# Two edits in a two-block network kernel: recurrent heads' maxima spread by DMA, attention heads' scores in pairs

## The chip, the cores and the metric

The kernel runs on one core of a Trainium2 chip. The metric is device time of one execution in microseconds (us). A core has TensorE (PE; its weight loads are PEld), VectorE (DVE), ScalarE (ACT), GpSimd (POOL) and SyncE (SP), which here only issues transfers.

## The reference

Two blocks over 256 tokens of width 1024, fp32, depth 2 each. What matters here is the attention of the first block and the recurrent mixer of the second. The rest (projections, gated feed-forward, stick-breaking attention, and a product-key expert layer) is untouched.

```python
# first block, both layers: 16 heads of 64, 4 key heads, band of 128, a sink per head
sc = einsum('bqkgd,bskd->bkgqs', q, k) * scale        # masked to the band
m = maximum(max(sc), sink)
p = exp(sc - m);  denom = sum(p) + exp(sink - m)
o = einsum('bkgqs,bskd->bqkgd', p / denom, v)

# second block, layer 0: 8 recurrent heads (mLSTM), queries and keys of 64, values of 128
b = cumsum(log_sigmoid(f_pre))
log_d = where(causal, b[l] - b[s] + i_pre[s], -inf)
m_t = maximum(b + m_prev, max(log_d))                 # the running maximum
s_qk = einsum('bhcld,bhcsd->bhcls', q, k) * exp(log_d - m_t)
hh = (s_qk @ v + ...) / maximum(abs(den), exp(-m_t))
```

## The kernel before

The kernel is traced in the order of the Python program; a planner then orders each engine's instructions by their place in the program and by when it reckons their inputs and buffers to be ready. So on each engine a later instruction can go ahead of an earlier one that has to wait. Waits between engines are set by the planner too; two instructions that touch one PSUM bank, one writing and one reading, are kept in program order.

**Projections.** Every weight block (128x1024, 512 KB) is loaded by SP (`load`, L166, 4 buffers `raw`), split into a high part by ScalarE (L177, `whi`, 5 buffers) and a residual by VectorE (L180, `wlo`, 5 buffers), and multiplied three times (`mm3`, L185 to L187: high by high, residual by high, high by residual). `form_b` makes a 128x256 result (PSUM tile mmB, 24 matmuls of 256 columns), `form_a` two 128x512 results (mmA). There are 4 PSUM buffers for these, 2 in the pool `pt` (tag "tp") and 2 in the pool `pa` (tag "sc").

**Attention (`_first_layer`, L390 to L446).** The work is cut into eight groups a layer: two halves of the tokens by four key heads, four query heads each. `scores(t, g)` makes, head by head, three matmuls over 64 partitions (L402; an even head's operands lie in partitions 0 to 63, an odd one's in 64 to 127) and a VectorE reduction that adds the band and takes the maximum (L405, into one of 6 buffers `e`). Two consecutive heads (0 and 1, 2 and 3) share one PSUM tile sc of `pa`. `values(t, g)` takes the exponentials (L417), divides (L421), transposes (L427), splits (L429, L430) and multiplies by the values into the tile po, also of `pa`; L436 and L437 put the result into oThi and oTlo. Scores of one group are traced ahead of the values of the one before. The convolution's projections (L456 on) do not depend on the attention; the mix (L477 on) reads oThi and oTlo.

**Recurrent heads (`mlstm`, L581).** The three gate columns g3 of each head are transposed to 8 partitions, where VectorE's scans make the running maxima M (8 heads x 128 tokens, two halves, L660 to L665). Eight projections with a convolution and a SiLU make queries and keys (L674 to L684), a `form_a` the second half of the values (L698). Then `head` runs eight times: tile pe takes minus M on all 128 partitions (L705: a fp32 matmul of a one-row selector by M) plus the causal mask (L706: a bf16 identity by the mask), in the pool `pt`; three exponentials (L710) make the weights me from pe and the gates; the scores mps (L713, L714, pool `pa`) are multiplied in by VectorE (L716); the values mpo (L718 to L720, pool `pa`) are copied (L722) and squared (L724). After the heads come the output gate's projections (L744) and the output projection.

A matmul on fp32 tiles appears as two instructions, on the split tiles as one.

Of the kernel before, what the change touches and what calls it, by code (L numbers as in the profile page):

```python
# [7 lines left out]
F32 = mybir.dt.float32  # L8
BF16 = mybir.dt.bfloat16
# [3 lines left out]
AF = mybir.ActivationFunctionType  # L13
ALU = mybir.AluOpType
# [3 lines left out]
S = 256  # L18
# [15 lines left out]
NEG = -1e30  # L34


def bc(ap, shape):
    return ap.to_broadcast(shape)
# [77 lines left out]
class Net:  # L116
# [66 lines left out]
    def mm3(self, out, lhs, rhs, start, stop):  # L183
        nc = self.nc
        nc.tensor.matmul(out, lhsT=lhs[0], rhs=rhs[0], start=start, stop=False)  # L185
        nc.tensor.matmul(out, lhsT=lhs[0], rhs=rhs[1], start=False, stop=False)  # L186
        return nc.tensor.matmul(out, lhsT=lhs[1], rhs=rhs[0], start=False, stop=stop)  # L187

    def pop(self):
        self.done += 1  # L190
# [134 lines left out]
    def _first_layer(self, ctx, l, norm, nxt, setup):  # L325
        nc, tc, d = self.nc, self.tc, self.d
# [63 lines left out]
        def scores(t, g):  # L390
            mx = self.sm.tile([128, 4], F32, tag="mx", name="mx")
            nm = self.sm.tile([128, 4], F32, tag="nm", name="nm")
            sk = self.sm.tile([128, 4], F32, tag="sk", name="sk")
            dn = self.sm.tile([128, 4], F32, tag="dn", name="dn")
            scs = []
            for i in range(4):
                hh = 4 * g + i
                r0 = 64 * (hh % 2)
                if i % 2 == 0:
                    sc2 = self.pa.tile([128, 2, S], F32, tag="sc", name="sc")  # L400
                sc = sc2[:, i % 2, :]
                self.mm3(sc, [v[r0:r0 + 64, hh // 2, t * 128:(t + 1) * 128] for v in qT],  # L402
                         [v[r0:r0 + 64, g, :] for v in kT], True, True)
                e = B.tile([128, S], F32, tag="e", name="e", bufs=6)
                nc.vector.tensor_tensor_reduce(e, sc, self.band[:, t, :], 1.0, NEG, op0=ALU.add, op1=ALU.max,  # L405
                                               accum_out=mx[:, i:i + 1])
                scs.append(e)
            sv = sink[:, 4 * g:4 * g + 4]
            nc.vector.tensor_tensor(mx, mx, sv, op=ALU.max)
            nc.vector.tensor_scalar(nm, mx, -1.0, None, op0=ALU.mult)  # L410
            nc.vector.tensor_tensor(sk, sv, mx, op=ALU.subtract)
            return nm, sk, dn, scs
# [168 lines left out]
    def mlstm(self, norm, g1, nxt):  # L581
        nc, tc, d = self.nc, self.tc, self.d
        with ExitStack() as ctx:
# [11 lines left out]
            le = A.tile([128, 128], F32, name="le")  # L595
            gt = A.tile([128, 128], F32, name="gt")
            mkf = A.tile([128, 128], F32, name="mkf")
            mk = A.tile([128, 128], BF16, name="mk")
            idb = A.tile([128, 128], BF16, name="idb")
            sel = A.tile([8, 8, 128], F32, name="sel")  # L600
            nc.sync.dma_start(le, d["c_le"])
            nc.sync.dma_start(gt, d["c_gt"])
            nc.sync.dma_start(mkf, d["c_mk_gt"])
            nc.vector.tensor_copy(mk, mkf)
            nc.vector.tensor_copy(idb, self.ident)
            nc.sync.dma_start(sel, d["c_sel"])
            one = A.tile([128, 1], F32, name="one")
            nc.vector.memset(one, 1.0)

# [46 lines left out]
                nc.tensor.transpose(p3[0:8, j, :], g3[:, j, :], self.ident)  # L656
            s3 = A.tile([8, 3, 128], F32, name="s3")
            nc.vector.tensor_copy(s3, p3[0:8, 0:3, :])
            M = A.tile([8, 3, 128], F32, name="M")
            nc.vector.tensor_tensor_scan(M[:, 0, :], s3[:, 0, :], s3[:, 0, :], 0.0, op0=ALU.max, op1=ALU.max)  # L660
            in1 = A.tile([8, 1], F32, name="in1")
            nc.vector.tensor_reduce(in1, s3[:, 2, :], axis=AX.X, op=ALU.max)
            nc.vector.tensor_tensor(in1, in1, beta, op=ALU.max)
            nc.vector.tensor_tensor_scan(M[:, 1, :], s3[:, 1, :], s3[:, 1, :], in1, op0=ALU.max, op1=ALU.max)
            nc.vector.tensor_copy(M[:, 2, :], M[:, 1, :])  # L665
            em = A.tile([128, 2, 8], F32, name="em")
            p4 = self.pt.tile([128, 4, 128], F32, tag="tp", name="tp4")
            for t in range(NT):
# [32 lines left out]

            def head(hh):
                r0, c = 64 * (hh % 2), hh // 2
                pe = self.pt.tile([128, 3, 128], F32, tag="tp", name="pe")
                nc.tensor.matmul(pe, lhsT=sel[:, hh, :], rhs=M, start=True, stop=False)  # L705
                nc.tensor.matmul(pe[:, 0:3:2, :], lhsT=idb, rhs=bc(mk[:, None, :], [128, 2, 128]),  # L706
                                 start=False, stop=True)
                e = B.tile([128, 3, 128], F32, tag="me", name="me")
                for j, g in ((0, 0), (1, 2), (2, 1)):
                    nc.scalar.activation(e[:, j, :], pe[:, j, :], AF.Exp, bias=g3[:, g, hh:hh + 1])  # L710
                psx = self.pa.tile([128, 3, 128], F32, tag="sc", name="mps")
                q, k = qk[c], qk[4 + c]
                nc.tensor.matmul(psx[:, 0:2, :], lhsT=k[r0:r0 + 64, 0:128], rhs=q[r0:r0 + 64, :], start=True, stop=True)  # L713
                nc.tensor.matmul(psx[:, 2, :], lhsT=k[r0:r0 + 64, 128:256], rhs=q[r0:r0 + 64, 128:256],  # L714
                                 start=True, stop=True)
                nc.vector.scalar_tensor_tensor(e, psx, 0.125, e, op0=ALU.mult, op1=ALU.mult)  # L716
                po = self.pa.tile([128, 2, 129], F32, tag="sc", name="mpo")
                nc.tensor.matmul(po[:, 0, :], lhsT=e[:, 0, :], rhs=va[0][:, hh, :], start=True, stop=True)  # L718
                nc.tensor.matmul(po[:, 1, :], lhsT=e[:, 1, :], rhs=va[0][:, hh, :], start=True, stop=False)
                nc.tensor.matmul(po[:, 1, :], lhsT=e[:, 2, :], rhs=va[1][:, hh, :], start=False, stop=True)  # L720
                for t in range(NT):
                    nc.vector.tensor_copy(num[t][:, hh, :], po[:, t, :])  # L722
                    jk = B.tile([128, 128], F32, tag="mjk", name="mjk")
                    nc.scalar.activation(jk, po[:, t, 0:128], AF.Square, accum_out=ss[t][:, hh:hh + 1])  # L724
# [438 lines left out]
def layout(inp):  # L1163
# [54 lines left out]
    if "ma_w_in_2" in inp:  # L1218
        w = f("ma_w_in_2")
        cat["ma_w_qk"] = tile_b(w[:, :, :1024])[0]  # L1220
        cat["ma_w_vo"] = tile_a(w[:, :, 1024:3072])[0]
        wif = np.zeros((128, KD, 128), np.float32)
        wif[:, :, :16] = w[0, :, 3072:].reshape(KD, 128, 16).transpose(1, 0, 2)
        cat["ma_w_if"] = wif.reshape(128, D)
        cat["ma_conv_w"] = np.ascontiguousarray(f("ma_conv_w_2")[0].reshape(4, KD, 128).transpose(2, 1, 0).reshape(128, 4 * KD))
        cat["ma_b_if"] = f("ma_b_if_2")
        cat["ma_hnorm_g"] = f("ma_hnorm_g_2").reshape(1, D)
        cat["ma_w_out"] = tile_a(f("ma_w_out_2"))[0]
        cat["c_le"] = (p <= q).astype(np.float32)
        cat["c_gt"] = (p > q).astype(np.float32)  # L1230
        cat["c_mk_gt"] = np.where(p > q, NEG, 0.0).astype(np.float32)
        sel = np.zeros((8, 8, 128), np.float32)
        sel[np.arange(8), np.arange(8)] = -1.0
        cat["c_sel"] = sel
    if "kv_w_2" in inp:
        cat["kv_ada_w"] = np.ascontiguousarray(f("kv_ada_w_2").T.reshape(1, 16, 128, D))
        cat["kv_ada_b"] = fm(f("kv_ada_b_2")[None])
# [99 lines left out]
```

## Time and profile before

| | us |
|---|---|
| median of the timed runs (3) | 2929.24 |
| lowest, highest | 2927.11, 2933.46 |
| the profiled execution | 2919.5 |
| its span, first to last instruction | 2917.7 |

| engine | busy us | share of the span |
|---|---|---|
| TensorE matmul (PE) | 2878.2 | 99% |
| TensorE weight load (PEld) | 2589.4 | 89% |
| VectorE (DVE) | 2163.6 | 74% |
| ScalarE (ACT) | 1433.5 | 49% |
| GpSimd (POOL) | 145.3 | 5% |

Matmuls are pipelined: one appears as busy from its start to the end of its drain, and the next has started by then. So the busy share of PE only says that its queue never ran dry; what a matmul costs is the step from its start to the next one's. "PEclk" is the granted TensorE clock as a share of 2.4 GHz: 1.00 is 2.4, 0.50 is 1.2 GHz.

### The profile page before, as it was taken

Reading aid. Unit: us, or ns where it says so; the run is one execution under the profiler, and the core shown is the slowest. Engines: PE = TensorE matmul, PEld = TensorE weight load, DVE = VectorE, ACT = ScalarE, POOL = GpSimd, SP = SyncE. Lnnn points to the kernel's source line nnn. Section 1 sums busy time; section 2 is a strip of 40 time slices with the busy share of each in tenths; the row PEclk is TensorE's granted clock in tenths of the full one; section 3 lists DMA queues with packets and bytes.
Section 4 is the critical chain, followed back from the end, with each engine's and each line's share of the span. In section 5 each row is a group of like instructions: output and inputs, shape, how many; then the busy total and the mean of one; then the engine's idle time right before and its main releaser. Section 6 shows DMA issues by size and latency. Waiting matters only on the chain.

```text
span 2917.7 us, 50501 instructions
## 1 busy us (share of the span) xinstructions
PE 2878.2 (99%) x19693; PEld 2589.4 (89%) x19693; DVE 2163.6 (74%) x4179; ACT 1433.5 (49%) x2363; POOL 145.3 (5%) x54
## 2 busy tenths in 40 slices
PE   8999999999999999999999999999999999999999
PEld 7898997899897789999999887877899999988887
DVE  6886766886755576978876897686599787569865
ACT  6645445554545564453344334566544434443454
POOL 0000000000000002330000000000032200000000
PEclk9999999999999899999999999999999999999999
DMA  6385775367665345564588358753455545554564
GB/s 216 104 284 190 262 250 192 109 222 241 224 199 182 125 152 157 183 211 142 171 278 270 122 172 281 229 183 115 137 162 172 183 140 159 188 167 128 188 201 146
DMA packets 153570, 542.40 MB, mean 186 GB/s; under 512 B 20002, under 2 KB 21226, under 8 KB 153330
## 3 DMA queue, kind: packets, MB, share of 16 engines
q1 hardware_dynamic: 153330, 539.18, 57.2%
q8 instruction: 154, 2.52, 0.3%
q14 instruction: 86, 0.70, 0.1%
HBM read 538.02 MB, written 1.09 MB: 185 GB/s over the span
## 4 chain that ended last, share of the span: by engine, by line
PE 89%; DVE 8%; ACT 1%; DMA 1%; issue 1%; SPq 0%; DVEq 0%; ACTq 0%
PE acc L185 8%; PE acc L187 8%; PE acc L186 8%; PE mmB L186 7%; PE mmB L187 7%; PE mmB L185 7%; PE pA L185 6%; PE pA L186 6%; PE pA L187 6%; PE mmA L186 5%; PE mmA L187 5%; PE mmA L185 5%; PE pG L968 4%; DVE wlo L180 2%; PE sc L185 1%
## 5 line engine op out<-in xcount | busy, mean ns | idle before, releaser
L177 ACT CAST whi<-raw 128x1024 fp32r<-128x1024 f32 x893 | 936.0, 1050 | 866.9 <-PE pA L186 364.5
L180 DVE TENSOR_TENSOR wlo<-raw,whi 128x1024 fp32r<-128x1024 f32 x849 | 1048.7, 1240 | 336.5 <-ACT whi L177 332.9
L185 PE MATMUL pA<-hhi,whi 128*128 128x256 f32 x2048 | 585.6, 286 | 5.7 <-ACT act L917 4.8
L186 PE MATMUL pA<-hlo,whi 128*128 128x256 f32 x2048 | 579.2, 283 | 0.0
L187 PE MATMUL pA<-hhi,wlo 128*128 128x256 f32 x2048 | 578.9, 283 | 0.0
L186 PE MATMUL mmB<-hlo,whi 128*128 128x256 f32 x1480 | 423.2, 286 | 0.0
L187 PE MATMUL mmB<-hhi,wlo 128*128 128x256 f32 x1480 | 421.6, 285 | 0.0
L185 PE MATMUL mmB<-hhi,whi 128*128 128x256 f32 x1480 | 421.5, 285 | 0.0
L187 PE MATMUL acc<-whi,wr 128*128 128x512 f32 x1024 | 400.4, 391 | 2.6 <-DVE wr L989 2.4
L185 PEld LDWEIGHTS pA<-hhi,whi 128*128 128x128 f32 x2048 | 393.4, 192 | 9.7 <-ACT act L917 5.9
L186 PE MATMUL acc<-wlo,wr 128*128 128x512 f32 x1024 | 401.0, 392 | 0.0
L186 PEld LDWEIGHTS pA<-hlo,whi 128*128 128x128 f32 x2048 | 392.4, 192 | 2.2
L185 PE MATMUL acc<-whi,wr 128*128 128x512 f32 x1024 | 393.2, 396 | 0.0
L187 PEld LDWEIGHTS pA<-hhi,wlo 128*128 128x128 f32 x2048 | 392.2, 191 | 0.0
L186 PEld LDWEIGHTS mmB<-hlo,whi 128*128 128x128 f32 x1480 | 282.9, 191 | 4.3
L187 PEld LDWEIGHTS mmB<-hhi,wlo 128*128 128x128 f32 x1480 | 282.8, 191 | 2.3
L185 PEld LDWEIGHTS mmB<-hhi,whi 128*128 128x128 f32 x1480 | 282.9, 191 | 1.5
L988 ACT CAST wr<-act 128x256 fp32r<-128x256 f32 x256 | 103.6, 406 | 346.1 <-PE acc L186 340.9
L187 PEld LDWEIGHTS acc<-whi,wr 128*128 128x128 f32 x1024 | 192.2, 188 | 46.9 <-DVE wr L989 6.6
L186 PEld LDWEIGHTS acc<-wlo,wr 128*128 128x128 f32 x1024 | 192.6, 188 | 39.1 <-DVE wlo L180 0.6
L185 PEld LDWEIGHTS acc<-whi,wr 128*128 128x128 f32 x1024 | 193.1, 189 | 35.6 <-ACT wr L988 0.2
L537 DVE CUSTOM_DVE_ANT_0 adaw<-adaw,cb 128x1024 f32<-128x1024 f32 x112 | 136.9, 1223 | 86.4 <-DMA adaw<-in_ada_w 77.5
(357 smaller groups left out, 4063.1 us busy)
## 6 DMA issues: line engine op xcount, KB each, us to landing
raw<-in_peer_u SPq DMA_DIRECT2D x256, 512.0 KB, 3.7
raw<-in_peer_v SPq DMA_DIRECT2D x256, 512.0 KB, 4.1
adaw<-in_ada_w SPq DMA_DIRECT2D x96, 512.0 KB, 4.7
raw<-in_w_gates SPq DMA_DIRECT2D x80, 512.0 KB, 3.9
raw<-in_w_down SPq DMA_DIRECT2D x44, 512.0 KB, 3.9
raw<-in_w_gate SPq DMA_DIRECT2D x36, 512.0 KB, 4.1
raw<-in_w_up SPq DMA_DIRECT2D x36, 512.0 KB, 4.0
raw<-in_w_qkv SPq DMA_DIRECT2D x24, 512.0 KB, 4.5
```

The source lines that it names most:

```text
L177: (nc.vector.tensor_copy if FIRST_HI[i:i + 1] == "v" else nc.scalar.copy)(hi, raw)
L180: self.last_lo = lo_eng.tensor_tensor(lo, raw, hi.bitcast(F32), op=ALU.subtract)
L185: nc.tensor.matmul(out, lhsT=lhs[0], rhs=rhs[0], start=start, stop=False)
L186: nc.tensor.matmul(out, lhsT=lhs[0], rhs=rhs[1], start=False, stop=False)
L187: return nc.tensor.matmul(out, lhsT=lhs[1], rhs=rhs[0], start=False, stop=stop)
L537: nc.vector.tensor_tensor_reduce(w, w, self.csilu, 1.0, 0.0, op0=ALU.mult, op1=ALU.add, accum_out=col[:, j:j + 1])
L968: nc.tensor.matmul(pg[:, :, 4 * g + t], lhsT=e2[:, g, :, t], rhs=e1[:, j, :, t], start=(j == 0), stop=(j == 1))
L988: nc.scalar.copy(gh, row(c))
```

## The change

In the attention, a group's two score tiles are made ahead of its reductions. `mm3_pair` takes two heads at a time, one in each half of the partitions, and alternates between them; the first of each pair writes tile 0 and the second tile 1, so that a tile now holds heads 0 and 2, or 1 and 3. The four reductions follow.

In the recurrent heads, M is stored to DRAM (8 KB) and loaded back to all 128 partitions in one transfer of 1 MB (Mb); VectorE subtracts the mask once for all heads (Mm, two instructions). The exponentials read Mm and Mb in SBUF, with a scale of -1. The matmuls L705 and L706 and what fed them go: the tile sel and its load, the bf16 copies of mask and identity, the copy of M's second half. The buffers me go from 2 to 4, and mpo moves to the pool `pt`, where pe was.

```diff
+    def mm3_pair(self, outs, lhss, rhss, start, stop):
+
+        for i, (a, b) in enumerate(((0, 0), (0, 1), (1, 0))):
+            for out, lhs, rhs in zip(outs, lhss, rhss):
+                self.nc.tensor.matmul(out, lhsT=lhs[a], rhs=rhs[b], start=start and i == 0, stop=stop and i == 2)
...
             scs = []
+            sc2 = [self.pa.tile([128, 2, S], F32, tag="sc", name="sc") for j in range(2)]
+            for i in range(2):
+                rs = [slice(64 * j, 64 * j + 64) for j in range(2)]
+                self.mm3_pair([sc2[j][:, i, :] for j in range(2)],
+                              [[v[r, 2 * g + i, t * 128:(t + 1) * 128] for v in qT] for r in rs],
+                              [[v[r, g, :] for v in kT] for r in rs], True, True)
             for i in range(4):
-                hh = 4 * g + i
-                r0 = 64 * (hh % 2)
-                if i % 2 == 0:
-                    sc2 = self.pa.tile([128, 2, S], F32, tag="sc", name="sc")
-                sc = sc2[:, i % 2, :]
-                self.mm3(sc, [v[r0:r0 + 64, hh // 2, t * 128:(t + 1) * 128] for v in qT],
-                         [v[r0:r0 + 64, g, :] for v in kT], True, True)
                 e = B.tile([128, S], F32, tag="e", name="e", bufs=6)
-                nc.vector.tensor_tensor_reduce(e, sc, self.band[:, t, :], 1.0, NEG, op0=ALU.add, op1=ALU.max,
-                                               accum_out=mx[:, i:i + 1])
+                nc.vector.tensor_tensor_reduce(e, sc2[i % 2][:, i // 2, :], self.band[:, t, :], 1.0, NEG, op0=ALU.add,
+                                               op1=ALU.max, accum_out=mx[:, i:i + 1])
...
-            mk = A.tile([128, 128], BF16, name="mk")
-            idb = A.tile([128, 128], BF16, name="idb")
-            sel = A.tile([8, 8, 128], F32, name="sel")
...
-            nc.vector.tensor_copy(mk, mkf)
-            nc.vector.tensor_copy(idb, self.ident)
-            nc.sync.dma_start(sel, d["c_sel"])
...
-            M = A.tile([8, 3, 128], F32, name="M")
+            M = A.tile([8, 2, 128], F32, name="M")
...
-            nc.vector.tensor_copy(M[:, 2, :], M[:, 1, :])
+            Md = self.dram.tile([8, 2, 128], F32, name="Md")
+            nc.sync.dma_start(Md, M)
+            Mb = A.tile([128, 8, 2, 128], F32, name="Mb")
+            Mm = A.tile([128, 8, 2, 128], F32, name="Mm")
+            nc.sync.dma_start(Mb.rearrange("p a b c -> p (a b c)"),
+                              bc(Md.rearrange("a b c -> (a b c)")[None, :], [128, 2048]))
+            for i in range(2):
+                v = slice(4 * i, 4 * i + 4)
+                nc.vector.tensor_tensor(Mm[:, v], Mb[:, v], bc(mkf[:, None, None, :], [128, 4, 2, 128]), op=ALU.subtract)
...
-                pe = self.pt.tile([128, 3, 128], F32, tag="tp", name="pe")
-                nc.tensor.matmul(pe, lhsT=sel[:, hh, :], rhs=M, start=True, stop=False)
-                nc.tensor.matmul(pe[:, 0:3:2, :], lhsT=idb, rhs=bc(mk[:, None, :], [128, 2, 128]),
-                                 start=False, stop=True)
-                e = B.tile([128, 3, 128], F32, tag="me", name="me")
-                for j, g in ((0, 0), (1, 2), (2, 1)):
-                    nc.scalar.activation(e[:, j, :], pe[:, j, :], AF.Exp, bias=g3[:, g, hh:hh + 1])
+                e = B.tile([128, 3, 128], F32, tag="me", name="me", bufs=4)
+                for j, g, m in ((0, 0, Mm[:, hh, 0]), (1, 2, Mb[:, hh, 1]), (2, 1, Mm[:, hh, 1])):
+                    nc.scalar.activation(e[:, j, :], m, AF.Exp, bias=g3[:, g, hh:hh + 1], scale=-1.0)
...
-                po = self.pa.tile([128, 2, 129], F32, tag="sc", name="mpo")
+                po = self.pt.tile([128, 2, 129], F32, tag="tp", name="mpo")
```

## Rows read from the trace of the kernel before

**Rows 1.** The page: chain that ended last, share of the span by engine

```profile
PE 89%; DVE 8%; ACT 1%; DMA 1%; issue 1%; SPq 0%; DVEq 0%; ACTq 0%
```

**Rows 2.** Attention by stretch: us; PE, PEld, DVE, ACT, POOL busy (instructions); PEclk; DMA

```profile
75.00:95.00 20.00, 19.95 (x146) 17.76 (x146) 17.00 (x58) 12.04 (x33) 0.00 (x0) 1.00 0.23 80
```

**Rows 3.** The same columns: recurrent heads, then the stick-breaking heads

```profile
993.00:1005.00 12.00, 12.00 (x34) 7.62 (x32) 2.28 (x7) 3.80 (x18) 0.00 (x0) 0.50 0.00 1
1995.00:2045.00 50.00, 50.00 (x248) 38.43 (x247) 30.08 (x55) 36.59 (x74) 0.00 (x0) 1.00 0.20 66
```

**Rows 4.** Instructions on tile sc: count, ns min/median/max, first and last start

```profile
L185 PE MATMUL sc<-kThi,qThi x64: 277/382/385, 55.1 to 594.1; 64*128 64x256 f32 x64
...
L405 DVE CUSTOM_DVE_ANT_0 e<-sc,band x64: 409/424/426, 57.7 to 595.1; 128x256 f32<-128x256 f32 x64
```

**Rows 5.** TensorE in order of time around one head: start us, us, instruction

```profile
89.74 0.28 PE L185 MATMUL mmB<-hhi,whi 128*128 128x256 f32 x1
89.95 0.38 PE L185 MATMUL sc<-kThi,qThi 64*128 64x256 f32 x1
...
90.50 0.39 PE L186 MATMUL mmB<-hlo,whi 128*128 128x256 f32 x1
...
90.83 0.28 PE L185 MATMUL mmB<-hhi,whi 128*128 128x256 f32 x1
```

**Rows 6.** The same view: head 0's last score matmul, then head 1's second

```profile
57.36 0.28 PE L187 MATMUL sc<-kThi,qTlo 64*128 64x256 f32 x1
57.48 0.28 PE L186 MATMUL sc<-kTlo,qThi 64*128 64x256 f32 x1
```

**Rows 7.** Recurrent heads by stretch, instructions on mmA alone: us; PE, PEld, DVE, ACT

```profile
985.10:1022.50 37.40, 4.79 (x15) 2.78 (x14) 0.00 (x0) 0.59 (x1) 0.63 0.15 53
```

**Rows 8.** TensorE in order of time, one period of the recurrent heads

```profile
1000.13 1.22 PE L713 MATMUL mps<-qkT,qkT 64*128 64x256 f32 x2
...
1001.70 0.40 PE L706 MATMUL pe<-mk,idb 128*128 128x256 bf16 x1
...
1003.60 0.80 PE L718 MATMUL mpo<-va,me 128*128 128x129 f32 x2
...
1005.19 1.22 PE L713 MATMUL mps<-qkT,qkT 64*128 64x256 f32 x2
```

**Rows 9.** The same view, an earlier head

```profile
990.54 0.49 PE L718 MATMUL mpo<-va,me 128*128 128x129 f32 x2
...
991.40 0.70 PE L713 MATMUL mps<-qkT,qkT 64*128 64x256 f32 x2
...
992.25 0.28 PE L706 MATMUL pe<-mk,idb 128*128 128x256 bf16 x1
```

**Rows 10.** ScalarE by line, 985 to 1022.6 us: count, busy us, mean ns, idle

```profile
L710 ACT ACTIVATE me<-pe,g 128x128 f32<-128x128 f32 x24 | 7.0, 368 | 5.9 <-PE pe L706 5.9
L724 ACT ACTIVATE mjk<-mpo 128x128 f32<-128x128 f32 x14 | 3.9, 281 | 16.8 <-DVE num L722 16.8
L724 ACT ACTIVATION_READ_ACCUMULATOR mjk<-mpo 128x1 f32 x14 | 2.9, 205 | 0.0
L710 ACT ACT_TABLE_LOAD x1 | 1.3, 1283 | 0.0
```

**Rows 11.** SP's queue in order of time: a store to DRAM and its reader

```profile
869.50 0.34 SPq L560 DMA_DIRECT2D rowsd<-rows  x1
...
871.26 0.33 SPq L57 DMA_DIRECT2D ab<-rowsd  x1
```

**Rows 12.** The page, costliest groups: the weights' residual

```profile
L180 DVE TENSOR_TENSOR wlo<-raw,whi 128x1024 fp32r<-128x1024 f32 x849 | 1048.7, 1240 | 336.5 <-ACT whi L177 332.9
```

**Rows 13.** By stretch, columns of rows 2: between the maxima and the heads

```profile
957.00:985.00 28.00, 28.00 (x191) 25.85 (x189) 24.10 (x50) 17.00 (x28) 0.00 (x0) 1.00 0.61 192
```

**Rows 14.** Instructions on tile oTlo, 54 to 170 us, columns of rows 4

```profile
L437 DVE TENSOR_TENSOR oTlo<-po,oThi x16: 408/416/419, 78.6 to 151.1; 64x256 fp32r<-64x256 f32 x16
...
L186 PE MATMUL mmB<-oTlo,whi x8: 277/280/285, 163.2 to 165.7; 128*128 128x256 f32 x8
```

More of the change, by code (lines that the diff above doesn't have):

```diff
@@ L1231, in layout @@
         cat["c_mk_gt"] = np.where(p > q, NEG, 0.0).astype(np.float32)
-        sel = np.zeros((8, 8, 128), np.float32)
-        sel[np.arange(8), np.arange(8)] = -1.0
-        cat["c_sel"] = sel
     if "kv_w_2" in inp:
```

## The prediction

> **What bounds the kernel now.** I read the chain of waits first: 89% of it is TensorE [rows 1]. So a microsecond taken from another engine is worth nothing until TensorE waits for it, and a microsecond of TensorE's own queue is worth about one. Then I looked at the two stretches that the change touches, with the views by stretch and in order of time. In the attention stage TensorE is busy for 19.95 of 20 us at full clock, while VectorE has 3.0 us to spare [rows 2]: score and value work takes turns with projections (tile mmB), which fill every gap. In the recurrent heads TensorE is also busy without a break, but at half the clock, with ScalarE at 3.8 of 12 us [rows 3]. Neither stage waits for a load or another engine; what counts is how long TensorE's own instructions stand in its queue.
>
> **Attention, what is there.** There are 64 heads' scores, three matmuls each over 64 partitions [rows 4]. A head is alone between projections over 128 partitions: the seven starts from 89.74 to 90.83 us make six steps, three of them scores [rows 5]. Steps inside one shape take 0.12 [rows 6], so six would be 0.71 us; the stretch takes 1.09. A visit to the 64-partition shape thus costs 0.38 us beside the work, about 0.19 on entry and on exit. Nearly every head pays it, since the second head of a tile writes the PSUM bank that VectorE reads for the first: its matmuls wait for that reduction, and the projections go between.
>
> **Attention, after.** The two tiles of a group are now in two banks and hold heads 0, 2 and 1, 3; all twelve matmuls come in the program ahead of the first reduction. Nothing is removed or added: twelve matmuls, four reductions. What goes is visits. If all twelve stand together there is one per group (16 in all, 48 fewer, 18 us); if each tile's six do, two (32 fewer, 12 us); if each pair of three and three breaks up again, nothing. The two buffers of that PSUM pool are shared with the value tile po, so one tile can often be filled before the other is free: I take two visits, 32 x 0.38 = **12 us**. The projections that stood between move up; they have to run anyhow, and VectorE has 15% left for their residuals [rows 2]. If that cover went, the most that could be lost is the 12 us.
>
> **Recurrent heads, what goes.** From 985.1 to 1022.5 us eight heads run, with 4.8 us of projections among them [rows 7], so 32.6 us are the heads'. One period is 5.06 us: the scores mps take 1.57, the two matmuls that spread the maxima and the mask (pe) 1.90, the values mpo 1.59 [rows 8]. The same pieces at full clock, before it falls, took 0.85 (mps) and 0.86 (mpo), the changes of shape at their ends within [rows 9]. Without pe a head is 1.71 us at full clock, 8 x 1.71 = 13.7, which saves 18.9; at half clock 3.16, 25.3 in all, which saves 7.3. Which clock? The granted clock is 0.50 in the stage as it is, where 8-partition, 64-partition and 128-partition matmuls alternate; in the later stick-breaking heads, 64-partition fp32 logits between 128-partition matmuls, it is 1.00 for 50 us at 100% busy [rows 3]. The new loop is nearest to these, so I take full clock.
>
> ScalarE then becomes the neighbour to watch: per head three exponentials of 0.37 and two squares of 0.28 + 0.20 [rows 10], 2.07 us against TensorE's 1.71. The exponentials no longer wait for TensorE, and four buffers let four heads' run early, so ScalarE's load within the stage is 8 x 0.96 + 12 x 0.37 = 12.1 plus a table load of 1.28, level with 13.7. What TensorE waits there is filled by output-gate projections that follow anyway. I take off 2 us for the start and the end of the loop: **17 us**. The source in SBUF instead of PSUM I cost at nothing: 24 instructions of 0.37, off TensorE's path.
>
> **What is added, and where it hides.** Two transfers and two subtractions, between the maxima (about 957 us) and the heads (985). The rows of the modulation show the same pattern: the store is issued at 869.50 and the load that reads it back at 871.26 [rows 11], so SP's queue stands for up to 1.8 us, with the weight loads behind it. The load here is 1 MB, twice the one there. Weights are loaded and cast up to nine buffers ahead (4 raw, 5 split), and SP mostly waits for a free one, so I take 0; if that cover is gone it is 1.8 us plus the transfer's share of the queues. The subtractions are 2 x 1024 elements a partition, 1.24 us each by the residual of the same size [rows 12]: 2.5 us where VectorE has 3.9 of 28 free [rows 13]. Cost 0; without the cover, 2.5. The copies and the load that are dropped are below 1 us, off the path.
>
> The early exponentials may fall among the eight SiLUs of the convolution, and each crossing of function sets costs two table loads of 1.28 [rows 10]. ScalarE has 11.0 us free there [rows 13], the exponentials take 4.4, so 6.6 us pay for two crossings; eight would overrun by 14 us. The weight casts come first in the program's order and run five projections ahead, 5 x 24 x 0.12 = 14 us, so I take 0, at worst 5.
>
> **Sum.** 12 + 17 = 29 us, against the profiled execution's 2919.5 (span 2917.7 and 1.8 around it): 2890.5. The median of the timed runs is 9.7 above that execution, so in timed terms 2929.2 - 29 = 2900.
>
> **Rivals.**
> 1. The two partition halves overlap. Paired matmuls alternate between partitions 0 to 63 and 64 to 127 and write two banks. Should a pair run at once, 192 matmuls of 0.12 would take half: 11.5 us more, 2929.2 - 40.5 = 2889. Against it: at 57.36 the last matmul of one half is followed by the first of the other, and the step is 0.12 as everywhere [rows 6], with the same bank written. Chance 0.15. The Trainium skill has a rule for this (TensorEngine Tiling (Array Packing), Key Properties): different tiles of the array can load weights and multiply in parallel. By that rule rival 1 would be the forecast; the one step in the trace doesn't agree with it, though not with two banks.
> 2. The clock stays at half in the recurrent heads: 12 + 7 = 19 us, 2910. For it: the 64-partition share of a head is larger than in the stick-breaking stage. Chance 0.15.
> 3. The pairs do not do what they say: the order still splits a group into four visits, 17 us only, 2912. For it: a matmul goes when its bank is free, and the two banks come free at different times. Chance 0.08.
> 4. Slower. Both score tiles now occupy both buffers until their second reductions, and po needs one. Now one group takes (151.1 - 78.6)/7.5 = 9.7 us, and the first reader of the result comes at 163.2, 12 us after the last piece [rows 14]. The shorter queue eats 6 of these per layer, 6 are left. If scores no longer run beside the previous group's values, a group grows by its scores and reductions: 12 x 0.12 + 0.38 + 4 x 0.42 [rows 4] = 3.5 us. Eight groups and two layers: 2 x (28 - 6) = 44 us of waiting, less the 29 gained: 2929 + 15 = 2944. It decides from 2.6 us a group: 2 x (8 x 2.6 - 6) = 29.6, all of the gain. Against it: the reduction of a tile's second head no longer waits for a matmul, which shortens the same chain by about a matmul group. Chance 0.08; 0.08 more for a growth near 2.6, which ends within 0.2%.
>
> **How the numbers follow.** The forecast has 0.46, rivals 1 to 3 have 0.38 together: faster by over 0.2% (5.9 us, about what a measurement of this kernel tells from no change) 0.84, within it 0.08, slower 0.08. The range takes in rival 1 with the spread of the timed runs below it (2882) and rival 3 with the 5 us of crossings above it (2918): 0.84 less a little at the edges.
>
> **What would show it.** Right: around a group of scores the rows show six or twelve matmuls at 0.12 with one entry and exit; L705 and L706 are gone; the granted clock is 1.00 through the heads; mps to mps is about 1.7 to 2.1 us with projections between; the stage is 15 to 18 us shorter. Wrong: steps under 0.10 in the pairs (rival 1); 0.50 in the stage (rival 2); lone triples (rival 3); a TensorE wait ahead of the first reader of oTlo, or groups over 10.5 us (rival 4); more than three table loads between 957 and 985 with TensorE waiting for casts.

## The result and the profile after

The changed kernel takes 2893.61 us (median; lowest 2893.22, highest 2895.06), the kernel before 2928.18 us on the same chip (2922.21 to 2933.46): a ratio of 0.9883, 95% interval 0.9867 to 0.9900. That is 34.6 us less by medians; the prediction was 2900, with 2882 to 2918 as its range. The profiled execution of the changed kernel took 2893.22 us (span 2891.4), 26.3 less than that of the kernel before (2919.5). The two differences are not the same because before's profiled execution lay 9 us under its own median and after's on it.

To see where the 26.3 us came from, I took the start of the n-th matmul on a tile in each trace and subtracted that of the same matmul in the trace of before. This shift, in us, at the times of before given at the top (the runs other than "after" are told of below):

| trace | 44 | 500 | 722 | 983 | 1050 | 1237 | 1300 | 2911 |
|---|---|---|---|---|---|---|---|---|
| after | 0.5 | -6.2 | -13.9 | -11.6 | -31.9 | -32.8 | -25.5 | -26.2 |
| attention alone | -0.4 | -7.7 | -15.4 | -12.9 | -13.2 | -13.5 | -13.6 | -14.0 |
| heads alone | -0.9 | -1.6 | -1.6 | 1.1 | -18.7 | -18.1 | -14.5 | -15.2 |
| SiLU later | 1.2 | -5.3 | -13.0 | -10.2 | -29.9 | -28.9 | -28.8 | -28.6 |
| exponentials later | 0.9 | -7.6 | -15.3 | -14.2 | -36.9 | -36.4 | -28.8 | -30.9 |
| pairs forced | 0.4 | -7.2 | -16.9 | -14.8 | -35.5 | -36.9 | -36.5 | -36.8 |
| all three | -0.4 | -9.9 | -19.6 | -17.2 | -39.9 | -41.2 | -40.7 | -40.3 |

From 44 to 722 lie the two attention layers (14.4 us gained), from 983 to 1050 the recurrent heads (20.3 gained), from 1237 to 1300 the first blocks of the product-key stage: there 7.3 us are lost, in a place that the change doesn't touch. Steps of one to three microseconds elsewhere mean little. Some come from short stretches in which the granted clock is 0.50 and which lie at other places in each trace: of the 2.3 us lost from 722 to 983, most goes with two of them in after (first two rows; the column behind the busy times is the clock), where before has none (third row):

```profile
725.20:728.20 3.00, 2.97 (x10) 2.20 (x9) 1.95 (x5) 2.29 (x8) 0.00 (x0) 0.50 0.87 333
919.60:922.80 3.20, 3.17 (x11) 2.38 (x10) 2.95 (x7) 2.07 (x6) 0.00 (x0) 0.50 0.81 223
722.00:983.00 261.00, 255.52 (x1645) 230.10 (x1644) 170.89 (x282) 137.78 (x229) 3.75 (x1) 1.00 0.62 201
```

**Attention.** The view by stretch, with the columns of [rows 2]:

```profile
75.00:95.00 20.00, 19.94 (x158) 18.53 (x157) 18.30 (x62) 12.96 (x33) 0.00 (x0) 1.00 0.43 131
```

TensorE starts 158 instructions in these 20 us, where it started 146. In order of time (start us, us, instruction, how many in a row), first most of a group at the start of a layer, then one tile of an ordinary group:

```profile
58.27 0.38 PE L193 MATMUL sc<-kTlo,qThi 64*128 64x256 f32 x2
58.50 0.28 PE L193 MATMUL sc<-kThi,qTlo 64*128 64x256 f32 x2
58.62 0.28 PE L193 MATMUL sc<-kThi,qThi 64*128 64x256 f32 x2
...
58.85 0.28 PE L193 MATMUL sc<-kThi,qTlo 64*128 64x256 f32 x2
59.06 0.38 PE L185 MATMUL mmB<-hhi,whi 128*128 128x256 f32 x1
...
78.11 0.38 PE L193 MATMUL sc<-kThi,qThi 64*128 64x256 f32 x1
78.33 0.28 PE L193 MATMUL sc<-kTlo,qThi 64*128 64x256 f32 x1
78.44 0.28 PE L193 MATMUL sc<-kThi,qTlo 64*128 64x256 f32 x1
...
78.80 0.28 PE L193 MATMUL sc<-kThi,qTlo 64*128 64x256 f32 x1
```

At 78.11 a tile's six matmuls stand together, 0.12 apart: one half of the partitions, one visit, the other tile at another time. Counted over a layer there are 16 visits instead of 32. At 58.27 the two halves alternate, and "x2" takes the same 0.12 as "x1" below: the second of a pair starts mostly 3 to 4 ns, at most 10, after the first. Of 96 score matmuls of a layer, 10 start so. The sum of the score matmuls' steps fell from 17.50 to 13.14 us a layer.

**Recurrent heads.** By stretch (columns of rows 2), then two heads in order of time:

```profile
957.00:985.00 28.00, 27.36 (x168) 23.00 (x167) 20.14 (x43) 27.63 (x65) 0.00 (x0) 1.00 0.37 114
973.00:990.00 17.00, 16.36 (x105) 13.09 (x103) 12.89 (x27) 14.75 (x51) 0.00 (x0) 1.00 0.36 104
```

```profile
973.50 0.71 PE L716 MATMUL mps<-qkT,qkT 64*128 64x256 f32 x4
974.03 0.40 PE L717 MATMUL mps<-qkT,qkT 64*128 64x128 f32 x4
975.06 0.49 PE L721 MATMUL mpo<-va,me 128*128 128x129 f32 x2 [0.64 <-DVE me L719]
```

The granted clock is 1.00 from end to end, where it was 0.50 [rows 3]. Eight heads' own steps add up to 10.95 us (mps 4.95, mpo 6.00); in before they were 33.15 (mps 10.71, mpo 10.82, pe 11.62). "x4" shows two heads' scores in one visit, an odd and an even one, and they overlap like the attention's pairs. ScalarE, which had 11 us free between the maxima and the heads [rows 13], is full: 27.63 of 28 us. What fills it (line, operation, count, busy us, mean ns, idle) stands in this view of ScalarE from 948.9 to 973 us:

```profile
L691 ACT ACT_TABLE_LOAD x5 | 6.4, 1283 | 0.1
L713 ACT ACT_TABLE_LOAD x4 | 5.1, 1283 | 0.1
...
L713 ACT ACTIVATE me<-Mm,g 128x128 f32<-128x128 f32 x4 | 1.5, 394 | 0.0
L678 ACT ACT_TABLE_LOAD x1 | 1.3, 1283 | 0.0
L713 ACT ACTIVATE me<-Mb,g 128x128 f32<-128x128 f32 x2 | 0.8, 403 | 0.0
```

Ten loads of a function set: one for an earlier exponential (L678), and nine as ScalarE goes back and forth between the SiLUs (L691) and the heads' exponentials (L713), six of which go ahead in twos.

**The loss.** ScalarE in order of time at 1250 us, and TensorE's matmul that follows:

```profile
1250.92 1.28 ACT L528 ACT_TABLE_LOAD   x1
1257.90 1.06 ACT L528 ACTIVATE cb<-cb 128x1024 f32<-128x1024 f32 x1 [5.70 <-DMA cb<-in_c]
1258.98 1.28 ACT L920 ACT_TABLE_LOAD   x1
1260.27 0.38 ACT L920 ACTIVATE act<-pA 128x256 f32<-128x256 f32 x1
```

```profile
1255.13 0.28 PE L187 MATMUL pA<-hhi,wlo 128*128 128x256 f32 x1
1260.71 0.58 PE L185 MATMUL pA<-hhi,whi 128*128 128x256 f32 x1 [5.30 <-ACT act L920]
1261.09 0.41 PE L186 MATMUL pA<-hlo,whi 128*128 128x256 f32 x1
```

In the product-key stage each block's result pA goes through a Gelu on ScalarE (L920), which frees pA's buffer. Between two of these stands the SiLU of cb (L528), for a modulation that comes much later, and it waits 5.7 us for its load. The Gelu behind it is late, TensorE is idle for 5.3 us, and its next 14 steps are 0.21 instead of 0.12: the granted clock is 0.50 until 1264. In before the same SiLU waited 2.27 us, TensorE 1.87 behind it, and the clock stayed at 1.00:

```profile
1284.94 1.06 ACT L523 ACTIVATE cb<-cb 128x1024 f32<-128x1024 f32 x1 [2.27 <-DMA cb<-in_c]
```

The SiLU is not all of it. Some 25 us earlier in after, a cast of weights on ScalarE waits 4.67 us for VectorE's routing work (oh), the Gelu behind it is late, and TensorE waits too:

```profile
1233.61 1.04 ACT L177 CAST whi<-raw 128x1024 fp32r<-128x1024 f32 x1 [4.67 <-DVE oh L1133]
```

```profile
1234.99 0.39 PE L185 MATMUL pA<-hhi,whi 128*128 128x256 f32 x1 [1.24 <-ACT act L920]
```

In all TensorE idles 7.0 us in this stretch, against 1.9 in before. So of the 7.3 us, 3.4 are the longer wait behind the SiLU, some 2 the clock after it, and 1.7 the other waits.

### The profile page after: what moved, and what is told of

It reads as the page before. It is cut to its first block, busy times and chain, and to the rows that moved or that the text cites. A ratio compares the mean times of both kernels' runs of the same rounds, so it can differ in the third digit from the quotient of the medians.

```text
span 2891.4 us, 50436 instructions
## 1 busy us (share of the span) xinstructions
PE 2846.0 (98%) x19669; PEld 2575.9 (89%) x19669; DVE 2168.8 (75%) x4178; ACT 1442.9 (50%) x2372; POOL 144.2 (5%) x54
## 4 chain that ended last, share of the span: by engine, by line
PE 86%; DVE 11%; ACT 1%; DMA 1%; issue 1%; SPq 0%; DVEq 0%; ACTq 0%
PE acc L185 8%; PE acc L187 8%; PE acc L186 8%; PE mmB L185 7%; PE mmB L186 7%; PE mmB L187 7%; PE pA L185 5%; PE pA L186 5%; PE pA L187 5%; PE mmA L185 5%; PE mmA L186 5%; PE mmA L187 5%; PE pG L971 4%; DVE wlo L180 3%; PE sc L193 1%
## 5 line engine op out<-in xcount | busy, mean ns | idle before, releaser
L177 ACT CAST whi<-raw 128x1024 fp32r<-128x1024 f32 x893 | 935.8, 1050 | 872.1 <-PE pA L186 358.2
```

Of the source, the lines that this page charges most:

```text
L177: (nc.vector.tensor_copy if FIRST_HI[i:i + 1] == "v" else nc.scalar.copy)(hi, raw)
```

## The experiments

**Each half of the change alone.** The kernel before with only the attention's edit, and with only the recurrent heads'.

> The kernel before with the attention half of the change alone; the recurrent heads spread their maxima by TensorE as before. My forecast for this half was 12 us (32 visits to the 64-partition shape saved, 0.38 each); the shift that the two profiled executions show over the two attention layers is 13 to 15. If the halves of the change are separate, this kernel is 12 to 15 us faster than before, and the recurrent heads stand at a granted clock of 0.50 as before. If the attention's gain was given back by a later wait it is 0 to 6 us faster only; if the pairs overlapped throughout it would be 23.

> The kernel before with the recurrent heads' half of the change alone; the attention scores head by head as before. Forecast for this half: 17 us at full clock, 7 at half clock. The shift of the profiled executions over the stage is 22.6, of which 7.2 are lost later, in the product-key stage, where a SiLU on ScalarE's queue waits for its load with a Gelu behind it. If that loss hangs on how early the stage is reached, it should show here too: 15 us faster in all. If it is a chance of the planner in the changed kernel alone, 22 us faster.

Before took 2930.84 us in these runs (in the three sets of runs told of here its median was 2930.84, 2927.57 and 2926.62, so a few us between kernels of different sets are settled by the traces, not by the medians). The attention alone took 2911.26 (ratio 0.9933, 0.9915 to 0.9952), the heads alone 2906.50 (0.9923, 0.9896 to 0.9951). By the traces, which the table gives, the attention's half is worth 15.0 us from 44 to 722 and ends at 14.0; its recurrent heads are as in before (a granted clock of 0.50 from 990 to 1005 us). The heads' half is worth 19.8 up to 1050 and loses 3.6 of it at 1237 to 1300. That loss is not the SiLU's, which waits 1.95 us there, less than in before: it is a cast that waits 4.90 us for VectorE's routing work as above, and a clock that falls after it:

```profile
1249.81 0.39 PE L185 MATMUL pA<-hhi,whi 128*128 128x256 f32 x1 [1.82 <-ACT act L915]
```

```profile
1250.90:1254.10 3.20, 3.20 (x17) 3.20 (x16) 3.20 (x6) 0.13 (x1) 3.20 (x1) 0.50 0.51 168
```

So the SiLU's long wait came with neither half alone: its load went 4.7 us ahead of it here, as in before, and 2.1 in after. In time the halves are 19.6 and 24.3 us faster, more than the traces and the expectations have, and add up to 43.9 us where the whole change has 34.6; 3.7 of these 9 us are the difference of the two losses, the rest I can't place: it is about the spread of single executions (before: 2921.30 to 2939.65 in these runs).

**The modulation's SiLU behind a later Gelu.**

```diff
-        nc.scalar.activation(cb, cb, AF.Silu)
+        if late: return          # the caller issues it behind the Gelu of a later block
...
+                    if c == FIN + 4:
+                        with tc.issue_after(mark[1].ins):
+                            self.ada_silu()
...
-                    spare()
+                    if c >= FIN + 4:
+                        spare()
```

> The changed kernel, with the SiLU of the next layer's modulation (tile cb) put in ScalarE's queue behind the Gelu of a later block, so that it no longer waits for its load ahead of a Gelu that TensorE needs. Theory one, that this wait took back 7 us of the gain (TensorE idle 5.3 us ahead of the block, then the clock at half for a while): 5 to 7 us faster than the changed kernel, 2887 to 2889. Theory two, that the shift there comes from weight loads or from the clock and the wait only coincides with it: within 2 us of the changed kernel.

2889.87 us (0.9860, 0.9829 to 0.9891), 3.7 under the changed kernel, with overlapping intervals. The stretch itself is plain in the trace, first after, then this kernel (columns of rows 2):

```profile
1245.00:1275.00 30.00, 24.70 (x193) 24.50 (x193) 14.56 (x19) 14.48 (x21) 4.98 (x2) 0.89 0.71 234
```

```profile
1245.00:1275.00 30.00, 29.93 (x250) 29.68 (x248) 16.00 (x23) 15.88 (x24) 10.19 (x4) 1.00 0.72 246
```

TensorE starts 250 matmuls instead of 193 in 30 us, and the shift stays at -28.9 and -28.8 across the stage: with the SiLU's wait, and the clock's fall behind it, the loss against before is gone. TensorE still idles 1.7 us there for other waits, about what the SiLU cost before. The edit also holds back by three blocks the background work that uses the SiLU's result (`spare`); its share was not tried alone, but the rows of after put TensorE's long wait down to the Gelu, and the Gelu's lateness to the SiLU's load.

**The heads' exponentials behind the last SiLU.**

```diff
-                for j, g, m in ((0, 0, Mm[:, hh, 0]), (1, 2, Mb[:, hh, 1]), (2, 1, Mm[:, hh, 1])):
-                    nc.scalar.activation(e[:, j, :], m, AF.Exp, bias=g3[:, g, hh:hh + 1], scale=-1.0)
+                with tc.issue_after(silu.ins):
+                    ...                # the same three
```

> The changed kernel, with the recurrent heads' exponentials held on ScalarE behind the last SiLU of the convolution, so that they no longer cross from one function set to the other among the SiLUs (ten table loads of 1.28 us between 949 and 973 us in the changed kernel). If these loads delay weight casts that TensorE waits for: up to 5 us faster. If ScalarE's queue there has no reader that waits (my prediction's term of 0): within 2 us. Against it stands that the early exponentials are then lost for the heads: ScalarE 2.07 us a head against TensorE's 1.7, at most 3 us slower.

2887.96 us (0.9851, 0.9819 to 0.9883), 5.6 under the changed kernel. Three table loads are left where ten were, as this view of ScalarE shows (948.9 to 973 us, columns as above):

```profile
L678 ACT ACT_TABLE_LOAD x1 | 1.3, 1283 | 0.0
L691 ACT ACT_TABLE_LOAD x1 | 1.3, 1283 | 0.0
L714 ACT ACT_TABLE_LOAD x1 | 1.3, 1283 | 0.0
```

From 983 to 1050 the shift grows by 22.7 instead of 20.3. The same pair of numbers comes from the other kernels: 22.7 to 23.2 in the three with this edit, 19.2 to 20.7 in the six others that have the changed heads without an added matmul. So the crossings cost some 2.5 us, and the rest of the 5.6 is spread. They are paid in the heads: the heads' own steps are 9.34 us here and 10.95 in after, and the wait ahead of the output gate's transposes is 0.2 us and 1.5. My argument against this edit, that ScalarE would then lag in the heads, fell.

**Both orders.**

> The changed kernel with both orders of the earlier runs: the exponentials of the recurrent heads behind the convolution's last SiLU, and the SiLU of the modulation behind a later Gelu. Alone the first was 5.6 us faster than the changed kernel, the second 3.7. If their gains are separate stretches (heads, product-key stage), they add: 9 to 11 us, 2882.5 to 2885. The trace of the first still shows the 7 us lost in the product-key stage, which speaks for more than the sum rather than less, 12 at most. If both act through one wait: 2888.

2887.35 us (0.9865, 0.9849 to 0.9882; before 2927.57): 6.3 under the changed kernel and 2.5 under the SiLU's edit alone, not the 9 to 11 expected. The trace has both gains (23.2 in the heads, 0.5 lost in the product-key stage, where the first edit alone lost 7.6), so it isn't that they act through one wait; the single runs' medians had some 3 us of spread in them.

**Pairs forced.** Two matmuls of 4 columns, one into each score tile, go ahead of a group, and all its score matmuls wait for both; their result is overwritten.

```diff
+            lead = [nc.tensor.matmul(sc2[j][:, 0, 0:4], lhsT=h[0][:, 0, 0:128], rhs=h[0][:, 0, 0:4], start=True,
+                                     stop=True) for j in range(2)]
             for i in range(2):
...
+                with tc.issue_after(lead[0].ins), tc.issue_after(lead[1].ins):
+                    self.mm3_pair(...)
```

> The changed kernel, with all twelve score matmuls of a group held behind two tiny leads (128x4, one in each of the two score tiles, overwritten at once), so that the planner can't place one tile's six ahead of the other's: pairs alternate between the partition halves in every group, not only in two of eight. Added work: 32 leads. In the changed kernel pairs that do alternate start 3 to 4 ns apart, 0.117 a pair; groups whose tiles stand apart take 0.12 a matmul. If the overlap is open to all groups, 0.7 to 0.85 us go in each of some 12 groups: 8 to 10 us faster than the changed kernel, 2884 to 2886. If waiting for both buffers costs what is won (my rival 4's mechanism), it is no faster, with TensorE waits ahead of the groups or the mix, up to 15 us slower.

2889.20 us (0.9879, 0.9863 to 0.9896), 4.4 under the changed kernel. An ordinary group of this kernel, in order of time, then its waits of TensorE from 40 to 180 us (total, times, longest):

```profile
77.45 0.20 PE L403 MATMUL sc<-hhi 128*128 128x4 f32 x1
...
83.65 0.27 PE L403 MATMUL sc<-hhi 128*128 128x4 f32 x1
83.86 0.39 PE L193 MATMUL sc<-kThi,qThi 64*128 64x256 f32 x2
84.08 0.28 PE L193 MATMUL sc<-kTlo,qThi 64*128 64x256 f32 x2
...
84.55 0.28 PE L193 MATMUL sc<-kThi,qTlo 64*128 64x256 f32 x2
```

```profile
PE po L185 <- DVE mx L413: 0.6, 3, 0.3
PE tpp L435 <- DVE e L429: 0.5, 1, 0.5
```

Twelve matmuls take 0.9 us instead of twice 0.9. The two leads of this group go 6.2 us apart (5.7 to 7.6 us in the first layer's ordinary groups): the two buffers were not to be had at one time. All 48 pairs of a layer overlap, and the score matmuls' steps fall from 13.14 to 7.43 us a layer, plus 1.86 for the leads: 3.85 less. The shift from 44 to 722 is -17.3, and -19.2 and -19.3 in two further kernels with this edit, against -14.2 to -16.2 in the eight without: against after's 14.4, 3 to 5 us for two layers, not 7.7, and not the 8 to 10 expected. Waits that were not there before take 1.1 us a layer; the first row is the start of rival 4's mechanism (po waits for a buffer that scores hold), and both together are a twentieth of the 22 us a layer that it was priced at. In this profiled execution the SiLU of cb waited only 1.7 us, and the 7 us in the product-key stage are missing from the loss (-36.9, then -36.5) though nothing there was edited.

**What the clock hangs on.** One fp32 matmul a head put back into the changed kernel, 256 columns, its result unread: once with the 8-partition selector (with its tile and its load), once over all 128 partitions.

```diff
+                pe = self.ps.tile([128, 2, 128], F32, tag="mm", name="pe")
+                nc.tensor.matmul(pe, lhsT=sel[:, hh, :], rhs=M, start=True, stop=True)             # first run
+                nc.tensor.matmul(pe, lhsT=self.ident, rhs=Mm[:, hh], start=True, stop=True)        # second run
```

> The changed kernel, with one matmul per recurrent head put back: the 8-partition fp32 selector by the maxima (256 columns, in a PSUM buffer of its own), whose result nothing reads. It tells what the clock's rise from 0.50 to 1.00 hangs on. If on the small matmuls: the granted clock falls to 0.50 or near it in the heads again and the stage grows by 10 to 15 us, 2903 to 2909. If on TensorE's time having been filled by other work (projections) or on the mask matmul: it stays at 1.00, and eight times two passes of 0.1 to 0.3 us and a change of shape cost 4 to 6 us, 2897 to 2900.

> The changed kernel, with one fp32 matmul per recurrent head put back that is like the selector of the earlier run in columns (256), passes, buffer and place, but works on all 128 partitions (the identity by Mm); its result is not read. With 8 partitions the granted clock fell to 0.54 in the heads and the stage grew by 19 us. If the 8 partitions are what the clock follows: 1.00 stays, and the stage grows by eight times two passes of 0.1 to 0.25 us and the changes of shape, 2 to 6 us, 2896 to 2900. If it is the added time outside projections, whatever its height: near 0.5 again, 2905 to 2912.

With 8 partitions: 2909.42 us (0.9942, 0.9922 to 0.9962), 15.8 over the changed kernel. With 128: 2892.59 (0.9883, 0.9866 to 0.9901), level with it, below the 2896 to 2900 expected: its stage is 3.6 us longer, but the product-key stage loses 3.6 us instead of 7.3. First the stretches and the added matmul (count, ns min/median/max, first and last start) of the run with 8 partitions, then those of the run with 128:

```profile
970.00:980.00 10.00, 10.00 (x37) 6.14 (x35) 4.97 (x9) 7.09 (x20) 0.00 (x0) 0.76 0.34 106
980.00:990.00 10.00, 10.00 (x27) 6.63 (x27) 4.22 (x8) 4.90 (x17) 0.00 (x0) 0.50 0.34 106
990.00:1000.00 10.00, 10.00 (x30) 7.11 (x30) 4.03 (x9) 1.36 (x8) 0.00 (x0) 0.50 0.16 52
1000.00:1005.00 5.00, 5.00 (x24) 4.37 (x23) 1.98 (x12) 1.77 (x11) 0.00 (x0) 0.74 0.01 3
```

```profile
L717 PE MATMUL pe<-M,sel x16: 374/629/789, 970.8 to 992.2; 8*128 8x256 f32 x16
```

```profile
970.00:980.00 10.00, 10.00 (x47) 7.04 (x45) 3.28 (x7) 9.18 (x22) 0.00 (x0) 1.00 0.01 3
980.00:990.00 10.00, 10.00 (x55) 7.98 (x54) 7.89 (x18) 8.22 (x30) 0.00 (x0) 1.00 0.53 160
```

```profile
L715 PE MATMUL pe<-Mm,ident x16: 377/379/483, 973.2 to 986.2; 128*128 128x256 f32 x16
```

TensorE is busy throughout in both. With the selector the clock falls within the first heads (970.8 is its first matmul) and is back some 10 us after the last (992.2); with 128 partitions it stays at 1.00. From 983 to 1050 the first gains 16.9 us less than after, the second 3.6, and the heads' steps, the added matmul's with them, are 29.3 and 17.7 us: 12 to 13 of the 17 are the clock's. So the selector alone, put back, is enough to bring the clock to half in this kernel, and added fp32 passes as such are not. The two matmuls differ in their data too (a selector of one row of -1 by the maxima, an identity by a full tile); a run that separates the height from the data was not made.

**The values' tile back in the pool of the scores.**

```diff
-                po = self.pt.tile([128, 2, 129], F32, tag="tp", name="mpo")
+                po = self.pa.tile([128, 2, 129], F32, tag="sc", name="mpo")
```

> The changed kernel, with the values' tile mpo of the recurrent heads back in the pool that the scores mps use (2 buffers), where it was before. In the changed kernel scores and values have two buffers each, and the scores of two heads run side by side. If that overlap or the freed buffers carry part of the 22 us of the heads: 3 to 6 us slower than the changed kernel. If the matmuls gone and the clock carry all: within 1.5 us of it.

2893.68 us (0.9891, 0.9874 to 0.9907): no difference. Two heads' scores no longer overlap (no steps below 30 ns, 12 in after), and the heads' own steps are 13.6 us instead of 10.95. But after's wait of 1.5 us ahead of the transposes of the output gate (tps behind VectorE's og) is gone from the list: the heads' end waits for VectorE's normalization, so 2.6 us of TensorE buy at most 1.1 (-19.2 against -20.3 from 983 to 1050).

**Together.** The three edits, and the same without the exponentials' order.

> The changed kernel with the three edits together: alternating pairs behind two leads per group, the exponentials behind the last SiLU, the modulation's SiLU behind a later Gelu. Measured alone, as medians: 4.4, 5.6 and 3.7 us faster than the changed kernel; the last two together 6.3. If the attention's gain (5 us by the traces) adds to these two: 2881 to 2884. If the spread of single executions of some 5 us made part of the earlier gains: 2885 to 2888.

> As the run with three edits, without the exponentials' delay. It tells whether that edit is worth anything beside the other two. If the table loads among the SiLUs cost TensorE 3 us, as the trace of the single run had it: 3 us slower than with all three. If that difference was spread: within 1.5 us of it, 2883 to 2887.

All three: 2881.06 us (2878.41 to 2883.01; before 2926.62; ratio 0.9844, 0.9829 to 0.9860). Without the exponentials' order: 2883.62 (0.9855, 0.9837 to 0.9874). The interval of the first lies below the changed kernel's: it beats both kernels, by some 12 us and 45 us. Between the two the difference of 2.6 us agrees with the 2.5 above, though the ranges overlap. By its trace all three gains are there: 19.2 us in the attention, 22.7 in the heads, 0.5 lost in the product-key stage.

## Why the prediction was right

Its mechanisms held, and its two terms were both too small, by 2.4 and 3.3 us; a loss of 7.3 us that it didn't see took back more than this surplus. That the time still came out some 6 us from the forecast is in part luck: by profiled executions it gained 3 us less than forecast, by medians 6 more.

- **What bounds the kernel.** Right. The chain of waits is still TensorE's, with VectorE's part grown a little (compare [rows 1]):

```profile
PE 86%; DVE 11%; ACT 1%; DMA 1%; issue 1%; SPq 0%; DVEq 0%; ACTq 0%
```

- **Attention, 12 us.** 14.4 measured, 15.0 in the half alone. Two visits per group came as forecast (16 a layer), and the leads of the forced run, some 6 us apart, fit the reason given: the two buffers come free at different times. The term that was short is overlap: 20 pairs in two layers at 0.117 are 2.3 us, and 14.4 - 2.3 = 12.1 is 32 visits at 0.38.
- **Recurrent heads, 17 us.** 20.3 measured. The clock rose to 1.00, as taken from the stick-breaking heads [rows 3], and the run with the selector showed that this was not luck: 8-partition matmuls bring 0.50 back. The size was off by 3.3. A head's own steps are 1.37 us, not 1.71, because two heads' scores share a visit and overlap, and start and end cost the 2 us taken off (waits of 0.6 and 1.5). But the two hang together: with the values' tile back the steps are 13.6 us, as forecast (13.7), nothing overlaps, and the stage still gains 19.2. So the overlap is worth 1.1 us at most, and without it the 2 us were hardly due.
- **ScalarE's crossings, 0, at worst 5.** Mis-sized: 2.5. The step that failed is "the weight casts come first in the program's order". The planner put exponentials among the SiLUs all the same, with ten loads where I allowed for two crossings, and ScalarE went from 17.00 busy us [rows 13] to 27.63. TensorE hardly waits there (0.64 us); the price falls in the heads, where fewer scores overlap and the end waits for VectorE. I had weighed only waiting casts.
- **Transfers, subtractions, the source in SBUF, 0.** Right. The store waits in SP's queue for the maxima, 2.3 us by the list of waits, a little over the 1.8 of [rows 11]; TensorE waits for no weight there. The load lands in 5.8 us. The subtractions took 1.22 each [rows 12], an exponential 0.394 instead of 0.368 [rows 10].

```profile
L713 ACT ACTIVATE me<-Mb,g x8: 389/398/407, 959.2 to 982.4; 128x128 f32<-128x128 f32 x8
L672 DVE TENSOR_TENSOR Mm<-Mb,mkf x2: 1217/1217/1217, 957.9 to 959.0; 128x1024 f32<-128x1024 f32 x2
```

- **Not seen: 7.3 us in the product-key stage.** The step that is missing: the sum let a gain run through to the end. But the moment at which work comes to a queue decides what it waits for there. A SiLU that waits for its load stood ahead of a Gelu in ScalarE's queue in before too. In before the load was issued 4.6 us ahead of the moment at which ScalarE was ready for the SiLU, which waited 2.27 us; in after 2.1 us ahead, and it waited 5.70; with the pairs forced it was 4.8 us ahead and waited 1.7. The clock's fall and the casts that wait for VectorE's routing work came on top.
- **The offset.** The sum was made against the profiled execution and moved to the median as it was, as if the 9.7 us between them would stay. By profiled executions 26.3 were gained of 29 forecast, by medians 34.6. The difference is 8 us of before's own spread, which after's executions (1.8 us apart) don't have. Of 28 timed executions of before, the seven fastest (2921 to 2924 us) have a mean granted clock of 0.993 or 0.994, as the profiled one (0.994), the five slowest (2932 us and more) 0.988 to 0.990, and those around the median mostly 0.991; after's have 0.995 or 0.996. An estimate from these: 0.003 less of 2920 us is some 17 us more at half the clock, 9 us of TensorE's time, about the whole offset. Why the clock differs from one execution to the next stays open.

**The rivals.** Rival 1, overlap of the halves: the mechanism is real, its reach was not. The rule of the Trainium skill that stood for it (TensorEngine Tiling (Array Packing), Key Properties) agrees with the trace: halves that alternate start mostly 3 to 4 ns apart. My evidence against it was one step of 0.12 between halves that wrote one bank [rows 6], and it says nothing on two banks. But the planner's order let 10 of 96 matmuls a layer have it, so the change gained 2.3 of the 11.5 us; forced, all 96 pairs of the two layers have it, and 96 x 0.117 = 11.2 is rival 1's sum, though the leads and the new waits kept most of what it adds from reaching the end. Whether one bank is what kept the halves apart in before was not tried. Rival 2 (clock at half) fell by 1.00 in every stretch, rival 3 (broken pairs) by the groups of six. Rival 4 (longer groups) fell: the groups take (144.6 - 73.7)/7.5 = 9.5 us where they took 9.7, and the first reader still comes 12 us after the last piece, as in [rows 14]:

```profile
L442 DVE TENSOR_TENSOR oTlo<-po,oThi x16: 405/417/421, 73.7 to 144.6; 64x256 fp32r<-64x256 f32 x16
...
L186 PE MATMUL mmB<-oTlo,whi x14: 277/280/285, 156.7 to 169.9; 128*128 128x256 f32 x14
```

## What to carry to other kernels

When TensorE bounds a kernel, look at what its small matmuls do to the rest: a visit to another tile shape cost 0.38 us here, for six matmuls as for three, and 8-partition matmuls between others held the granted clock at half for a whole stage. If work is made independent in order to pair or prefetch it, read in the next trace whether the planner put it where it pays: pairs need both buffers free at one time, and exponentials that may run early will run between functions of another set. And follow a gain to the end of the program: instructions that wait for a load or another engine in a shared queue took back 7 us here, at a place that nothing was changed in. And where medians and profiled executions give two different gains, compare the granted clocks of the executions first.

## What the runs showed of the hardware

- Matmuls on the two halves of the partitions that write two banks run at once when they are neighbours in TensorE's queue: mostly 3 to 4 ns from start to start on the split tiles, where a pair takes the 0.12 us of one, and about 14 ns for the fp32 scores of two recurrent heads.
- Sixteen 8-partition passes of 256 columns among others brought the granted clock from 1.00 to 0.50 with TensorE busy all the time; sixteen passes of the same length over 128 partitions left it at 1.00. Their data differ too.
- After 5.3 us of idleness, TensorE's steps from the second matmul on were 0.21 us instead of 0.12 for 14 matmuls (mean clock 0.89 over 30 us), so a wait of 5.3 us cost about 7. After a wait of 1.82 us the clock fell to 0.50 in the heads' half alone; after one of 1.87 in before it stayed at 1.00.
- A switch of ScalarE's function set costs 1.28 us: SiLU's end at 1258.96, load at 1258.98, Gelu at 1260.27.
